# Two-layer hybrid encoder in one kernel on one core: norm products, residual means, weight splits and the last transposes at other places in their engines' queues

## The chip, the core and the metric

The kernel runs on 1 core of one Trainium2 chip. Its engines each work through a queue of their own, in order: TensorE (PE, with its weight loads PEld), VectorE (DVE), ScalarE (ACT), GpSimd (POOL), and SyncE (SP), which issues most DMAs. The metric is the device time of one execution in microseconds (us); lower is better. Before the change the median of 3 runs is 2886.24 us (2885.1 to 2886.93).

## The reference, cut to what matters

Two layers over 1040 tokens (16 meta tokens and 1024 inputs) of width 1024. Layer 0 mixes tokens with a bidirectional S5 scan and a GLU, layer 1 with grouped-query attention. Each mixer is followed by a dense SwiGLU feed-forward part (width 2816), and each of the four parts ends in the same step:

```
x = layer_norm(alpha * x + f(x), gain, bias)      # mean and variance over the 1024 features of a token
```

The output is the last x without the 16 meta tokens.

## The kernel before, in words

Activations lie with features on partitions: `acc[:, k, tokens]` for eight feature tiles k, and 1040 tokens in three token tiles, 0 and 1 of 348 tokens and 2 of 344. Every product is made of three fp32r matmuls, from a high and a low half of both operands (L695, L696, L697); `Hh` and `Hl` are the halves of x, `unit` those of a weight block, `gt` those of the gated hidden values. One product group over eight feature tiles is 24 matmuls, one over the two hidden tiles of a chunk is 6. PSUM has eight banks, drawn from one pool (`bank()`).

The four norms are numbered `ln` 0 to 3: 0 behind the S5 part, 1 behind the first feed-forward part, 2 behind the attention, 3 behind the second feed-forward part, last. A norm works on one token tile. `ln_square` squares each finished feature tile on ACT (L722) and adds it on POOL into two partial sums s and q (`lns`, L724). `layer_norm` sums these over the partitions by two plain fp32 matmuls with a matrix of ones (L736, L737), the sums' products below; then ACT and DVE make the reciprocal root (L707 to L711), and for each feature tile DVE scales x (L751), ACT writes `Hh` (L752), DVE writes `Hl` (L746). After that `residual()` prepares the next residual sum: POOL adds the eight feature tiles (`lnz`, L765), PE makes their mean over partitions (L769), and DVE subtracts it from each feature tile (L772). The mean's bank is held until the eighth subtraction.

Such helper work is a generator. It is recorded between the product groups: each `yield` gives an amount of work, `group_done` counts it down (1.75 for each half of a 24-matmul group, 0.9 for a 6-matmul group), and the next piece is recorded when the count is used up. So the numbers behind `yield` fix where each piece stands in the queues of its engines; `flush` records what is left of a piece at once.

`Weights` streams 512 KB blocks of the weights: `dma` loads `raw`, and `split` turns a block into high and low halves. For most blocks ACT makes the high half (L610) and DVE the low half (L612); `on_pool` gives the low half of four blocks (the k and v weights of the attention) to POOL, also L612. The `down` blocks of a feed-forward part get their row means removed: ACT L607 and L617, DVE L618. `tick` makes the next split when a unit buffer is free.

A feed-forward part runs in eleven chunks: gate and up groups for three token tiles, then eight `down` groups of 6 matmuls for each token tile, whose results DVE adds into `acc` (L880 in the first chunk, L882 in the others). At the end of the program, for each token tile, PE transposes x back in pieces of up to 128 tokens (L1535), DVE and ACT copy a half of each piece into `ot` (L1539, L1537; three buffers), and SP sends it out.

Of the kernel before, what the change touches and what calls it, by code (L numbers as in the profile page):

```python
# [9 lines left out]
FP32 = mybir.dt.float32  # L10
# [3 lines left out]
ALU = mybir.AluOpType  # L14
# [24 lines left out]
class Pools:  # L39


    def __init__(self, tc):
        self.tc = tc
        self.open = {}
# [69 lines left out]
def s5_phase(nc, tc, P, a, ident, acc, xres, ydram, late):  # L114
# [180 lines left out]
    G3 = [tab2.tile([128, T, G], FP32, name=f"G{i}") for i in range(3)]  # L295
    E3 = [tab.tile([128, T, G], FP32, name=f"E{i}") for i in range(3)]
    fw, bw = slice(0, 64), slice(64, 128)
# [77 lines left out]

    def E(c2, g):
        return Eh[2 * g // G][:, c2, g % (G // 2)]
# [42 lines left out]
    def inside(gb):  # L420
# [7 lines left out]
        for j in range(NB):  # L428
            g = NB * gb + j
            for c2, src in enumerate((Br, Bi)):  # L430
                for d in range(2):
                    r = slice(64 * d, 64 * d + 64)
                    PE.matmul(b[32 * d:32 * d + CH, j * 128:(j + 1) * 128], src[r, g],
                              E(c2, g)[r].rearrange("p s c -> p (s c)"), start=(c2 == 0), stop=(c2 == 1))
        yield 6
# [92 lines left out]
    for ft in range(KT):  # L528
        for g0 in range(8 * ft, 8 * ft + 8, 2):
            b = bank()  # L530
            for j in range(2):
                g = g0 + j
                for c2 in range(2):
                    PE.matmul(b[:, j * NK:(j + 1) * NK], E(c2, g).rearrange("p s c -> p (s c)"), XS[:, :, c2, g],  # L534
                              start=(c2 == 0), stop=(c2 == 1))
# [31 lines left out]
class Weights:  # L567


    def __init__(self, nc, n_units, n_raw):  # L570
        self.nc, self.nu, self.nr = nc, n_units, n_raw
        self.src = []
        self.centre = {}
        self.on_pool = set()
        self.raw = []
        self.unit = []
        self.free = []
        self.base = 0
        self.limit = 10 ** 6
# [18 lines left out]
    def split(self):  # L598
        n = len(self.unit)
        self.dma()  # L600
        r = self.raw[n]
        u = self.up[(n - self.base) % self.nu // (self.nu // 2)].tile([128, 2, 1024], FP32R, tag="unit", name="unit")
        A, V = self.nc.scalar, self.nc.vector
        c = self.centre.get(n, False)
        if c is None:
            m = self.rp.tile([128, 1], FP32, tag="mean", name="mean")
            A.activation(out=u[:, 1], in_=r, func=ACTF.Copy, scale=-1.0 / 1024, accum_out=m)  # L607
            c = m
        if c is False:
            A.copy(out=u[:, 0], in_=r)  # L610
            E = self.nc.gpsimd if n in self.on_pool else V
            E.tensor_tensor(out=u[:, 1], in0=r, in1=u[:, 0].bitcast(FP32), op=ALU.subtract)  # L612
        else:
            w = 1024 // c.shape[1]
            for i in range(c.shape[1]):
                x = slice(w * i, w * i + w)
                A.activation(out=u[:, 0, x], in_=r[:, x], func=ACTF.Identity, bias=c[:, i:i + 1])  # L617
                V.scalar_tensor_tensor(out=u[:, 1, x], in0=r[:, x], scalar=c[:, i:i + 1], in1=u[:, 0, x].bitcast(FP32),  # L618
                                       op0=ALU.add, op1=ALU.subtract)
        self.unit.append(u)  # L620
        self.dma()

    def tick(self):
        n = len(self.unit)
        if n < min(len(self.src), self.limit) and (n < self.nu or self.free[n - self.nu]):
            self.split()

# [26 lines left out]
class Net:  # L654
    def __init__(self, nc, tc, P, a):
        self.nc, self.tc, self.P, self.a = nc, tc, P, a
        self.bg = []
        self.ln_s = {}


# [15 lines left out]
    def start(self, gen, key):  # L676
        it = [gen, 0, key]
        self.bg.append(it)
        self.bg_step(it)
        return it  # L680

    def flush(self, key):
        for it in list(self.bg):
            while it[2] == key and it in self.bg:
                self.bg_step(it)
# [40 lines left out]
    def layer_norm(self, tok, ln, last=False, save=None):  # L726
        nc = self.nc
        V, A, PE, PO = nc.vector, nc.scalar, nc.tensor, nc.gpsimd
        t0, n = TOK[tok]
        acc = self.acc  # L730
        x = [acc[:, k, t0:t0 + n] for k in range(KT)]
        tp = self.ln_p
        s, q2 = self.ln_s[tok, 0], self.ln_s[tok, 1]
        yield (3,3,3)[tok] if ln == 1 else 3.0
        v = self.bank()[:, :n]
        PE.matmul(v, self.ones, s, start=True, stop=False)  # L736
        PE.matmul(v, self.ones, q2, start=False, stop=True)  # L737
        A.preload_act_table_set("natural_log_exp_and_others")
        u = self.rstd(v, self.eps_ln, n, tp)

        def bias(k):
            return self.small[:, 32 + 8 * ln + k:32 + 8 * ln + k + 1]

        def finish(k):
            if not last:
                V.scalar_tensor_tensor(out=self.Hl[:, k, t0:t0 + n], in0=x[k], scalar=bias(k),  # L746
                                       in1=self.Hh[:, k, t0:t0 + n].bitcast(FP32), op0=ALU.add, op1=ALU.subtract)

        for k in range(KT):
            g = self.small[:, 8 * ln + k:8 * ln + k + 1]  # L750
            V.scalar_tensor_tensor(out=x[k], in0=x[k], scalar=g, in1=u, op0=ALU.mult, op1=ALU.mult)  # L751
            A.activation(out=x[k] if last else self.Hh[:, k, t0:t0 + n], in_=x[k], func=ACTF.Identity, bias=bias(k))  # L752
            if k > 1:
                finish(k - 2)
            if k % 2:
                yield 1.8
        finish(KT - 2)
        finish(KT - 1)

        def residual():  # L760

            yield (20.,20.,20.)[tok] if ln == 1 else 28.0
            sz = tp.tile([128, 348], FP32, tag="s", name="lnz", bufs=2)[:, :n]
            for k in range(1, KT):
                PO.tensor_tensor(out=sz, in0=x[0] if k == 1 else sz, in1=x[k], op=ALU.add)  # L765
                yield 0.9
            yield 4.0
            mz = self.bank()[:, :n]
            PE.matmul(mz, self.ones, sz, start=True, stop=True)  # L769
            for k in range(KT):  # L770
                b = self.bias_c[:, 8 * ln + k:8 * ln + k + 1]
                V.scalar_tensor_tensor(out=x[k], in0=x[k], scalar=b, in1=mz, op0=ALU.add, op1=ALU.subtract)  # L772
                yield 0.9
            if save is not None:
                nc.gpsimd.dma_start(out=save.rearrange("(k p) t -> p k t", p=128)[:, :, t0:t0 + n],
                                    in_=acc[:, :, t0:t0 + n])

        if not last:
            self.start(residual(), ("lnb", tok))
# [452 lines left out]
def whole(nc, tc, a, out):  # L1232
    P = Pools(tc)
    N = Net(nc, tc, P, a)
    V, A, PE, PO = nc.vector, nc.scalar, nc.tensor, nc.gpsimd
# [18 lines left out]
    w = N.w = Weights(nc, NU, NR)  # L1254
# [13 lines left out]
    wq = a["attn_w_qkv"][0]  # L1268
    uk = N.add_square(wq, 1024)
    uv = N.add_square(wq, 1280)  # L1270
    w.on_pool.update((uk + uv)[:4])
    uq = [N.add_square(wq, 256 * i) for i in range(2)]
    uv2 = N.add_square(wq, 1280)
    uq += [N.add_square(wq, 256 * i) for i in range(2, 4)]
# [250 lines left out]
    for t in range(3):  # L1525
        N.flush(("ln", t))
        t0, n = TOK[t]
        c0 = max(t0, 16)
        while c0 < t0 + n:
            m = min(128, t0 + n - c0)  # L1530
            ot = outp.tile([128, D], FP32, tag="ot", name="ot")
            for h in range(2):
                b = N.bank()
                for f in range(4):
                    PE.transpose(b[:m, f * 128:(f + 1) * 128], acc[:, 4 * h + f, c0:c0 + m], ident)  # L1535
                if h:
                    A.copy(out=ot[:m, 512:], in_=b[:m])  # L1537
                else:
                    V.tensor_copy(out=ot[:m, :512], in_=b[:m])  # L1539
            nc.sync.dma_start(out=out[0, c0 - 16:c0 - 16 + m, :], in_=ot[:m])  # L1540
            c0 += m
# [48 lines left out]
```

## Time and profile before

| | |
|---|---|
| median of 3 runs | 2886.24 us |
| the profiled execution | 2882.8 us, its span 2881.0 us |
| PE busy share of the span | 92% |
| DVE, ACT, POOL busy share | 55%, 41%, 19% |
| mean granted TensorE clock | 0.962 |

Times of the trace count from the start of the span. The S5 part ends at about 329 us, its output products and norm 0 at about 530, the first feed-forward part at about 1288, the attention at about 2000, the second feed-forward part at about 2845. A granted clock of 0.5 is the lower of TensorE's two levels (1.2 GHz), 1.0 the upper (2.4 GHz).

### The profile page before, as it was taken

Reading aid. Unit: us, or ns where it says so; the run is one execution under the profiler, and the core shown is the slowest. Engines: PE = TensorE matmul, PEld = TensorE weight load, DVE = VectorE, ACT = ScalarE, POOL = GpSimd, SP = SyncE. Lnnn points to the kernel's source line nnn. Section 1 sums busy time; section 2 is a strip of 40 time slices with the busy share of each in tenths; the row PEclk is TensorE's granted clock in tenths of the full one; section 3 lists DMA queues with packets and bytes.
Section 4 is the critical chain, followed back from the end, with each engine's and each line's share of the span. In section 5 each row is a group of like instructions: output and inputs, shape, how many; then the busy total and the mean of one; then the engine's idle time right before and its main releaser. Section 6 shows DMA issues by size and latency. Waiting matters only on the chain.

```text
span 2881.0 us, 43478 instructions
## 1 busy us (share of the span) xinstructions
PE 2660.3 (92%) x17277; PEld 2560.6 (89%) x17277; DVE 1586.5 (55%) x3270; ACT 1168.4 (41%) x2170; POOL 545.2 (19%) x544
## 2 busy tenths in 40 slices
PE   6654999999999999998999998999999999999997
PEld 5544899999999999998988888888999999999996
DVE  8897353743333333338768888886473333333334
ACT  6545442532212221244558777775432121222225
POOL 3771142400000000024014443431230000000002
PEclk8776999999999999999999999999999999999998
DMA  5111664121111111101201011112111111111101
GB/s 131 28 36 31 192 208 148 52 81 45 45 45 52 52 52 52 45 30 65 99 12 41 21 38 49 23 23 90 34 47 45 51 44 52 45 45 45 44 30 59
DMA packets 124839, 167.44 MB, mean 58 GB/s; under 512 B 13499, under 2 KB 104971, under 8 KB 124635
## 3 DMA queue, kind: packets, MB, share of 16 engines
q1 hardware_dynamic: 118203, 141.22, 17.2%
q0 software_dynamic: 5712, 21.30, 2.2%
q8 instruction: 136, 2.23, 0.3%
q10 hardware_dynamic: 720, 2.13, 0.2%
q14 instruction: 68, 0.56, 0.1%
HBM read 126.41 MB, written 21.23 MB: 51 GB/s over the span
## 4 chain that ended last, share of the span: by engine, by line
PE 77%; DVE 14%; ACT 4%; issue 3%; DMA 1%; POOL 1%; SPq 0%; ACTq 0%; POOLq 0%; DVEq 0%
PE bk L696 21%; PE bk L695 21%; PE bk L697 21%; PE pv L1107 4%; PE pt L1085 3%; DVE mx L1065 2%; DVE pl L1098 2%; PE b L534 2%; DVE IN L509 2%; DVE TA L507 2%; DVE XS L511 2%; ACT ph L1093 1%; DVE acc L751 1%; ACT P L1069 1%; PE bk L917 1%
## 5 line engine op out<-in xcount | busy, mean ns | idle before, releaser
L695 PE MATMUL bk<-Hh,unit 128*128 128x348 f32 (+1 forms) x2928 | 956.1, 327 | 7.4 <-ACT Hh L785 3.8
L696 PE MATMUL bk<-Hl,unit 128*128 128x348 f32 (+1 forms) x2928 | 945.3, 323 | 1.3 <-DVE Hl L789 1.0
L697 PE MATMUL bk<-Hh,unit 128*128 128x348 f32 (+1 forms) x2928 | 943.7, 322 | 0.0
L695 PEld LDWEIGHTS bk<-Hh,unit 128*128 128x128 f32 x2928 | 555.1, 190 | 12.6 <-ACT vf L1477 3.8
L696 PEld LDWEIGHTS bk<-Hl,unit 128*128 128x128 f32 x2928 | 554.8, 189 | 6.8 <-DVE Hl L789 2.4
L697 PEld LDWEIGHTS bk<-Hh,unit 128*128 128x128 f32 x2928 | 554.7, 189 | 0.0
L859 DVE TENSOR_TENSOR sg<-sg,bk 128x348 f32<-128x348 f32 x132 | 68.0, 515 | 631.7 <-PE bk L697 623.9
L724 POOL TENSOR_TENSOR lns<-lns,lnsq 128x348 f32<-128x348 f32 (+1 forms) x72 | 70.0, 982 | 1550.9 <-ACT lnsq L722 1549.8
L695 PE MATMUL bk<-gt,unit 128*128 128x348 f32 (+1 forms) x1056 | 340.3, 322 | 0.0
L697 PE MATMUL bk<-gt,unit 128*128 128x348 f32 (+1 forms) x1056 | 338.9, 321 | 0.0
L696 PE MATMUL bk<-gt,unit 128*128 128x348 f32 (+1 forms) x1056 | 338.3, 320 | 0.0
L882 DVE TENSOR_TENSOR acc<-acc,bk 128x348 f32<-128x348 f32 (+1 forms) x480 | 237.3, 512 | 112.5 <-PE bk L697 112.5
L861 ACT CAST gt<-sg 128x348 fp32r<-128x348 f32 x132 | 63.6, 482 | 490.0 <-DVE sg L859 490.0
L1085 PE MATMUL pt<-ident,P 128*116 128x128 f32 (+1 forms) x1188 | 181.6, 279 | 44.0 <-DVE pl L1098 38.7
L1098 DVE TENSOR_TENSOR pl<-pt,ph 116x512 fp32r<-116x512 f32 (+3 forms) x340 | 204.2, 618 | 15.1 <-ACT ph L1093 13.1
L1073 POOL TENSOR_SCALAR P<-P,l 128x1044 f32<-128x1044 f32 x132 | 149.9, 1148 | 293.3 <-PE pv L1107 170.0
L1085 PEld LDWEIGHTS pt<-ident,P 128*116 128x116 f32 (+1 forms) x1188 | 132.7, 136 | 80.5 <-issue 32.4
L696 PEld LDWEIGHTS bk<-gt,unit 128*128 128x128 f32 x1056 | 198.7, 188 | 0.5 <-issue 0.2
L695 PEld LDWEIGHTS bk<-gt,unit 128*128 128x128 f32 x1056 | 198.7, 188 | 0.5 <-issue 0.2
L610 ACT CAST unit<-raw 128x1024 fp32r<-128x1024 f32 x110 | 113.1, 1046 | 211.1 <-DMA raw<-in_ffn_w_up_dram 166.2
L1093 ACT CAST ph<-pt 116x512 fp32r<-116x512 f32 (+3 forms) x340 | 168.7, 535 | 73.9 <-PE pt L1085 59.8
L697 PEld LDWEIGHTS bk<-gt,unit 128*128 128x128 f32 x1056 | 198.6, 188 | 0.0
(286 smaller groups left out, 4053.7 us busy)
## 6 DMA issues: line engine op xcount, KB each, us to landing
raw<-in_ffn_w_gate_dram SPq DMA_DIRECT2D x44, 512.0 KB
raw<-in_ffn_w_up_dram SPq DMA_DIRECT2D x44, 512.0 KB
raw<-in_ffn_w_down_dram SPq DMA_DIRECT2D x44, 512.0 KB
y<-xdram SPq DMA_DIRECT2D x16, 520.0 KB
QA<-QH SPq DMA_DIRECT2D x30, 260.0 KB
raw<-in_attn_w_qkv_dram SPq DMA_DIRECT2D x14, 512.0 KB
xdram<-acc SPq DMA_DIRECT2D x32, 130.0 KB
xres<-xn POOLq DMA_DIRECT2D x8, 520.0 KB, 5.1
```

The source lines that it names most:

```text
L610: A.copy(out=u[:, 0], in_=r)
L695: mm(out, wh, xh, start=(first and i == 0), stop=False)
L696: mm(out, wh, xl, start=False, stop=False)
L697: mm(out, wl, xh, start=False, stop=(last and i == n - 1))
L724: (nc.vector if on_dve else nc.gpsimd).tensor_tensor(out=part, in0=part, in1=sq, op=ALU.add)
L859: V.tensor_tensor(out=sg, in0=sg, in1=bu, op=ALU.mult)
L882: V.tensor_tensor(out=x, in0=x, in1=b, op=ALU.add)
L1073: PO.tensor_scalar(out=k.P, in0=k.P, scalar1=k.l, scalar2=1.0, op0=ALU.mult, op1=ALU.mult)
L1085: PE.transpose(b[:m, w * i + 128 * x:w * i + 128 * x + 128], u.P[x][:, KB_N * kt:KB_N * kt + m], self.ident)
L1093: A.copy(out=u.ph[s][:m, :w], in_=u.t[s][:m, :w])
L1098: V.tensor_tensor(out=u.pl[s][:m, :w], in0=u.t[s][:m, :w], in1=u.ph[s][:m, :w].bitcast(FP32), op=ALU.subtract)
L1107: PE.matmul(u.o[:, :u.w], VAs[u.j][:m, kt], (u.ph, u.pl)[x][s][:m, c:c + u.w], start=(kt == 0 and x == 0), stop=(kt == KBS - 1 and x == 1))
```

## The change

Six edits. The sums' products of token tile 2 come later: norms 0 and 2 wait for 7.0 units of work in place of 3.0 (24 matmuls further on), norms 1 and 3 for 5.0 (12 matmuls further on). While norm tile 2 waits for these products, `hold` keeps `tick` from splitting a `down` block. The residual mean starts after 46, 38 and 28 units for tiles 0, 1, 2 of norms 0 and 2 (28 each before), and after 28, 26 and 22 for norm 1 (20 each before). The four low halves on POOL go to DVE. In the last stage `begin` records the sums' products of tile 2 behind the first piece of tile 1, in place of behind its third.

```diff
@@ class Weights
-        self.on_pool = set()
+        self.hold = False
@@ split
-            E = self.nc.gpsimd if n in self.on_pool else V
-            E.tensor_tensor(out=u[:, 1], in0=r, in1=u[:, 0].bitcast(FP32), op=ALU.subtract)
+            V.tensor_tensor(out=u[:, 1], in0=r, in1=u[:, 0].bitcast(FP32), op=ALU.subtract)
@@ tick
         n = len(self.unit)
+        if self.hold and n in self.centre and self.centre[n] is None:
+            return
@@ class Net
+        self.begun = []
...
+    def begin(self, key):
+
+        for it in list(self.bg):
+            if it[2] == key and it[1] > 0 and it not in self.begun:
+                self.begun.append(it)
+                self.bg_step(it)
@@ layer_norm
-        yield (3,3,3)[tok] if ln == 1 else 3.0
+        self.w.hold = tok == 2
+        yield 3.0 if tok < 2 else 5.0 if ln % 2 else 7.0
         v = self.bank()[:, :n]
         PE.matmul(v, self.ones, s, start=True, stop=False)
         PE.matmul(v, self.ones, q2, start=False, stop=True)
         A.preload_act_table_set("natural_log_exp_and_others")
         u = self.rstd(v, self.eps_ln, n, tp)
+        self.w.hold = False
@@ residual
-            yield (20.,20.,20.)[tok] if ln == 1 else 28.0
+            yield ((46.0, 38.0, 28.0), (28.0, 26.0, 22.0))[ln % 2][tok]
@@ whole
-    w.on_pool.update((uk + uv)[:4])
@@ the last stage
         while c0 < t0 + n:
+            if t == 1 and c0 > t0:
+                N.begin(("ln", 2))
```

On ACT, at the start of the first feed-forward part (the second starts alike), the rows before are these; `unit,mean` is the row mean of a `down` block, `rs_y` and `rs_u` belong to the norm of tile 2 (344 tokens), `sg` and `gt` to the gate of tile 0 (348):

```order
L607 ACTIVATE unit,mean<-raw 128x1024
L617 ACTIVATE unit<-raw,mean 128x1024
L607 ACTIVATE unit,mean<-raw 128x1024
L617 ACTIVATE unit<-raw,mean 128x1024
L738 ACT_TABLE_LOAD
L707 ACTIVATE rs_y<-bk,eps_ln 128x344
L708 ACTIVATE rs_y<-rs_y 128x344
L709 ACTIVATE rs_u<-rs_y 128x344
L752 ACTIVATE Hh<-acc,small 128x344 x4
```

and in the changed kernel:

```order
L607 ACTIVATE unit,mean<-raw 128x1024
L616 ACTIVATE unit<-raw,mean 128x1024
L869 ACT_TABLE_LOAD
L869 ACTIVATE sg<-bk 128x348
L872 CAST gt<-sg 128x348
L748 ACT_TABLE_LOAD
L716 ACTIVATE rs_y<-bk,eps_ln 128x344
L717 ACTIVATE rs_y<-rs_y 128x344
L718 ACTIVATE rs_u<-rs_y 128x344
L763 ACTIVATE Hh<-acc,small 128x344 x2
L607 ACTIVATE unit,mean<-raw 128x1024
L616 ACTIVATE unit<-raw,mean 128x1024
```

The first gate and up groups now stand ahead of the norm of tile 2, with a table load of their own, and the second `down` block is split behind its first `Hh`.

On DVE, where the first `down` groups of that part begin (`acc<-acc,bias_c,bk` is a subtraction of the residual mean, `acc<-acc,bk` the addition of a `down` result), the rows before are:

```order
L772 SCALAR_TENSOR_TENSOR acc<-acc,bias_c,bk 128x348 x7
L859 TENSOR_TENSOR sg<-sg,bk 128x344
L862 TENSOR_TENSOR gt<-sg,gt 128x344
L772 SCALAR_TENSOR_TENSOR acc<-acc,bias_c,bk 128x348
L880 SCALAR_TENSOR_TENSOR acc<-acc,bk 128x348 x4
L612 TENSOR_TENSOR unit<-raw,unit 128x1024
L880 SCALAR_TENSOR_TENSOR acc<-acc,bk 128x348 x4
L612 TENSOR_TENSOR unit<-raw,unit 128x1024
```

and in the changed kernel:

```order
L783 SCALAR_TENSOR_TENSOR acc<-acc,bias_c,bk 128x348 x2
L870 TENSOR_TENSOR sg<-sg,bk 128x344
L873 TENSOR_TENSOR gt<-sg,gt 128x344
L783 SCALAR_TENSOR_TENSOR acc<-acc,bias_c,bk 128x348 x6
L891 SCALAR_TENSOR_TENSOR acc<-acc,bk 128x348 x4
L611 TENSOR_TENSOR unit<-raw,unit 128x1024
L783 SCALAR_TENSOR_TENSOR acc<-acc,bias_c,bk 128x348
L891 SCALAR_TENSOR_TENSOR acc<-acc,bk 128x348
L783 SCALAR_TENSOR_TENSOR acc<-acc,bias_c,bk 128x348
```

The subtractions of tile 0 move from the gate and up groups to the head of the `down` groups, and those of tile 1 stand among the `down` results: between the last `sg` of the gates and the `down` results of tile 2 there are 22 subtractions, where there were 9.

On ACT, at the end of the program, the rows before are these (`ot` are output pieces of token tile 1, the rest the norm of tile 2):

```order
L752 ACTIVATE acc<-acc,small 128x348 x2
L1537 COPY ot<-bk 128x512 x2
L1537 COPY ot<-bk 92x512
L738 ACT_TABLE_LOAD
L707 ACTIVATE rs_y<-bk,eps_ln 128x344
L708 ACTIVATE rs_y<-rs_y 128x344
L709 ACTIVATE rs_u<-rs_y 128x344
L752 ACTIVATE acc<-acc,small 128x344 x8
```

and in the changed kernel:

```order
L763 ACTIVATE acc<-acc,small 128x348 x2
L1549 COPY ot<-bk 128x512
L748 ACT_TABLE_LOAD
L716 ACTIVATE rs_y<-bk,eps_ln 128x344
L717 ACTIVATE rs_y<-rs_y 128x344
L718 ACTIVATE rs_u<-rs_y 128x344
L763 ACTIVATE acc<-acc,small 128x344 x2
L1549 COPY ot<-bk 128x512
L1549 COPY ot<-bk 92x512
L763 ACTIVATE acc<-acc,small 128x344 x6
```

The second and third piece's copies of tile 1 move from ahead of the norm of tile 2 to behind its second feature tile.

## Rows read from the trace of the kernel before

**Rows 1.** The page, part 1: busy time and share of each engine.

```profile
PE 2660.3 (92%) x17277; PEld 2560.6 (89%) x17277; DVE 1586.5 (55%) x3270; ACT 1168.4 (41%) x2170; POOL 545.2 (19%) x544
```

**Rows 2.** Waits of PE: line, waited for, us in total, times, longest.

```profile
PE bk L736 <- POOL lns L724: 11.7, 4, 4.7
...
PE bk L737 <- POOL lns L724: 6.7, 2, 3.3
...
PE bk L695 <- ACT vf L1477: 3.6, 1, 3.6
...
PE bk L696 <- DVE Hl L789: 1.0, 1, 1.0
```

**Rows 3.** Short windows: length, busy us of PE, PEld, DVE, ACT, POOL; granted clock.

```profile
330.20:333.60 3.40, 3.40 (x12) 3.40 (x13) 3.40 (x7) 3.40 (x8) 1.38 (x4) 0.50 0.77 97
...
388.20:391.60 3.40, 3.40 (x20) 3.00 (x19) 2.08 (x6) 2.49 (x7) 0.78 (x1) 1.00 0.62 173
538.40:541.80 3.40, 3.40 (x11) 2.92 (x11) 2.04 (x2) 3.35 (x5) 3.24 (x3) 0.50 0.03 7
...
1330.30:1337.10 6.80, 5.62 (x19) 5.62 (x20) 5.74 (x13) 4.25 (x10) 0.00 (x0) 0.50 0.00 1
2088.00:2094.80 6.80, 5.21 (x16) 4.74 (x17) 3.19 (x2) 6.68 (x9) 5.95 (x5) 0.50 0.30 90
```

**Rows 4.** Timeline of PE at the mean of x: start, us, instruction, idle before.

```profile
387.48 0.85 PE L1369 MATMUL bk<-sx,ones 128*128 128x348 f32 x2 [0.95 <-POOL sx L1362]
```

**Rows 5.** Timeline at the start of the first feed-forward part.

```profile
533.98 0.85 PE L736 MATMUL bk<-lns,ones 128*128 128x344 f32 x2 [1.20 <-POOL lns L724]
...
535.97 0.50 DVE L1398 SCALAR_TENSOR_TENSOR acc<-acc,bk 128x344 f32<-128x344 f32 x1
...
537.20 0.91 POOL L724 TENSOR_TENSOR lns<-lns,lnsq 128x344 f32<-128x344 f32 x1 [3.27 <-ACT lnsq L722]
...
538.16 1.34 PE L737 MATMUL bk<-lns,ones 128*128 128x344 f32 x2 [3.33 <-POOL lns L724]
```

**Rows 6.** Timeline: the end of norm 0, and the first product that reads it.

```profile
559.43 1.54 DVE L746 SCALAR_TENSOR_TENSOR Hl<-acc,small,Hh 128x344 fp32r<-128x344 f32 x3
...
567.77 0.32 PE L695 MATMUL bk<-Hh,unit 128*128 128x344 f32 x1
```

**Rows 7.** Windows by stage, columns as in rows 3.

```profile
583.40:606.80 23.40, 23.40 (x149) 23.20 (x148) 20.24 (x38) 6.57 (x9) 0.00 (x0) 1.00 0.41 137
...
1331.50:1400.00 68.50, 68.50 (x395) 63.73 (x396) 57.49 (x104) 34.45 (x70) 18.10 (x19) 0.96 0.31 101
```

**Rows 8.** Timeline of DVE where the first down groups begin.

```profile
585.19 0.57 DVE L772 SCALAR_TENSOR_TENSOR acc<-acc,bias_c,bk 128x348 f32<-128x348 f32 x1
585.68 1.36 DVE L880 SCALAR_TENSOR_TENSOR acc<-acc,bk 128x348 f32<-128x348 f32 x3
```

**Rows 9.** Timeline: low halves on DVE and POOL, norm 1, and the vf copy.

```profile
526.71 1.23 DVE L612 TENSOR_TENSOR unit<-raw,unit 128x1024 fp32r<-128x1024 f32 x1 [1.55 <-ACT unit L610]
...
1301.82 2.65 POOL L612 TENSOR_TENSOR unit<-raw,unit 128x1024 fp32r<-128x1024 f32 x1
...
1308.15 1.51 PE L736 MATMUL bk<-lns,ones 128*128 128x344 f32 x2 [4.54 <-POOL lns L724]
...
1331.07 0.35 ACT L1477 COPY vf<-bk 116x256 f32<-116x256 f32 x1
```

**Rows 10.** The chain that ended last, in the last stage.

```profile
2855.14 7.46 DMA out_dram<-ot
```

**Rows 11.** Timeline of the last stage.

```profile
2856.01 3.98 PE L1535 MATMUL bk<-ident,acc 128*128 128x128 f32 x18 [1.81 <-ACT acc L752]
...
2862.70 0.58 ACT L1537 COPY ot<-bk 92x512 f32<-92x512 f32 x1 [3.35 <-DMA out_dram<-ot]
2863.30 1.28 ACT L738 ACT_TABLE_LOAD   x1
...
2867.38 3.99 DVE L751 SCALAR_TENSOR_TENSOR acc<-acc,small,rs_u 128x344 f32<-128x344 f32 x8
```

## The prediction

> **What bounds the kernel now.** I read the page's busy shares first: PE is busy 2660.3 of 2881.0 us [rows 1], so only the holes of PE and the stretches at its lower clock can be won. The waits of PE then name the holes that the change touches. The sums' products wait for POOL's partial sums, 11.7 + 6.7 us in all, and one product waits 3.6 us for ACT's copy of `vf` [rows 2]. The timelines place them: 1.20 + 3.33 us at 534 [rows 5], as much again at the second feed-forward part, 4.7 us for norm 1's tile 1, 4.54 us for its tile 2 (11.7 = 1.2 + 1.2 + 4.7 + 4.5 and 6.7 = 3.3 + 3.3), and 3.6 us for `vf` behind that [rows 2, 9]. Short windows show the second price of a hole: behind the wait at 534 the granted clock is 0.50 for 3.4 us, behind its twin 6.8 us, behind the `vf` wait 6.8 us [rows 3], and each us at 0.50 loses half a us. Behind a wait of 0.95 us the clock stays 1.00 [rows 3, 4]; behind one of 1.0 us that follows another short one it falls [rows 2, 3]. The last stage is a chain of its own: a DMA of 7.46 us frees an `ot` buffer, a copy follows, and only behind that copy ACT starts the last norm [rows 10, 11].
>
> **Start of each feed-forward part (twice).** What releases the second sums' product is not moved: DVE's last addition ends at 536.5, POOL's last add at 538.1 [rows 5]. Between the last product of the part before and the sums there are now 48 matmuls in place of 24. 24 matmuls at full clock are 3.8 us (149 in 23.40 us are 0.157 us each [rows 7]). So of 1.20 + 3.33 = 4.53 us about 0.7 us is left. A wait of 0.7 us is below the 0.95 us behind which the clock stayed, so the 3.4 us at half clock go too and give back 1.7 us. Gain: 3.8 + 1.7 = 5.5 us. At the twin 6.8 us were lost to the clock; I count one 3.4 us stretch there as well, and keep the other 1.7 us for the range.
>
> The cover for the norm of tile 2 is the gate and up work of tiles 0 and 1. It ended at 559.43 + 1.54 = 561.0 and was first read at 567.77 [rows 6]. PE now comes to that read some 5.5 us earlier, at 562.3, and to its eighth feature tile 3.3 us later. So about 4.6 us of cover are left for ACT's and DVE's detours: a first gate's `sg` and `gt` ahead of the norm, and a table load of 1.28 us [rows 11] for it. I cost these at nothing.
>
> The Trainium skill speaks against that step: ScalarE: Activation LUTs, section Table sets: the hidden batching unit, wants activations batched by table set, and the change splits a batch, two loads of 1.28 us per part. The trace agrees with the price of a load and shows the cover above; what it would take if the cover failed is the third rival.
>
> **First `down` groups (twice).** Here the change takes back. From 583.40 to 606.80 DVE was busy 20.24 of 23.40 us [rows 7], with 9 subtractions of the residual mean; in the changed order the same stretch holds 22. One takes 585.68 - 585.19 = 0.49 us from start to start [rows 8], so DVE has 20.24 + 13 x 0.49 = 26.6 us of work in 23.4 us, 3.2 us too much. POOL's adds and the mean's product are earlier than these subtractions and are not the limit. Eight PSUM banks let PE run ahead, but a mean's bank stays held until its eighth subtraction, which is now the last thing on DVE ahead of tile 2's results. Ends: 0 (the banks cover it) and 3.2 + 1.7 = 4.9 us (waits over 1 us, and a stretch at half clock). I take 3.2 us, the overrun itself. Net per part: 5.5 - 3.2 = 2.3 us; two parts: 4.6 us.
>
> **Norm 1 and the k, v and q products.** The sums' products of tile 2 move 12 matmuls on, 1.9 us of PE work into a wait of 4.54 us [rows 9]. The mean of tile 0 moves 62 matmuls on and leaves its bank free for one product more, 3.8 us of work in front of the wait for `vf`. That copy also has two `Hh` of tile 2 fewer ahead of it, so the 3.62 us go, with 3.4 us for the clock [rows 2, 3, 9]. Gains: 1.9 + 3.6 + 3.4 = 8.9 us.
>
> Against that stand the four low halves. On POOL one takes 2.65 us at its longest and delays the partial sums; on DVE it takes 1.23 us, but DVE first stands idle 1.55 us for ACT's high half, with the `down` results and norm steps queued behind it [rows 9]. In the queue of tile 2's sums that is 2.8 us on DVE for 2.65 us on POOL, about even; for tile 1 too. I count 1.4 us of loss, one half's run behind the last result. Then DVE must catch up: from 1331.50 to 1400.00 it is busy 57.49 of 68.50 us [rows 7], and its work does not begin earlier, since norm 1's sums are ready no sooner. A PE that comes 7.5 us earlier meets that queue. Of 7.5 us I keep 2.0 us, about what the shift of the sums gives by itself. Ends: a loss as in the fourth rival, and the full 7.5 us.
>
> **The last stage.** 16 transposes of the second and third piece now stand behind the sums' products: of 18 in 3.98 us [rows 11], 16 x 0.21 = 3.3 us by the mean of the row. The sums then run at half clock, 2.7 us for four passes where two took 1.34 us [rows 5]: from 2859.99 - 3.3 = 2856.7 to 2859.4. More comes from ACT: the root starts there, at about 2859.4, no longer at 2863.30 + 1.28 = 2864.6 behind the copy that waits for the DMA. DVE's first scaling follows 2.8 us later (2867.38 - 2864.6), at 2862.2. Two feature tiles, 1.0 us; then two copies into `ot` of 0.6 us each, the second of which is free at 2862.6; then six tiles at 0.5 us: 2867.4, where it was 2867.38 + 3.99 = 2871.4. Gain: 4.0 us. The two copies also start their DMAs later; if one takes 7.46 us again [rows 10], the last copy waits about 1.5 us. I take 3.5 us; ends 1.0 and 5.2 us (2864.6 - 2859.4).
>
> **Sum.** 4.6 + 2.0 + 3.5 = 10.1 us. The profiled execution took 2882.8 us (span 2881.0 and 1.8 us around it), so it would take 2872.7. The median of the runs shown lies 3.4 us above the profiled execution; the same offset gives 2876.1, and I predict 2876.
>
> **Rivals.**
> 1. The subtractions eat the gain. Both feed-forward parts lose 4.9 of their 5.5 us, norm 1 gives nothing, the last stage 2.2 us: 3.4 us, 2882.8. For it: DVE's 26.6 us against 23.4. Against: eight banks of lead.
> 2. All comes in full: 5.5 and 7.2 us, no overrun, 7.5 us in norm 1, 5.2 us at the end: 25.4 us, 2861. Against: DVE's 57.49 of 68.50 us, and the overrun.
> 3. The norm of tile 2 is late at the new place. Two loads of 1.28 us per part beyond the cover of 4.6 us cost 2.6 us twice: 10.1 - 5.2 = 4.9 us, 2881.3. Against: the cover.
> 4. Slower. The four low halves block DVE: each 1.55 + 1.23 = 2.8 us, together 11.1 us in front of the `down` results on which both waits of norm 1 hang, and each wait, then over 7 us, is followed by a further 3.4 us lost to the clock: 17.9 us. With 8.1 us won elsewhere this is 9.8 us slower, 2896. It decides if POOL's relief (four times up to 2.65 us) doesn't shorten the waits; below about 8 us of exposed halves the whole is not slower. Against: both waits end on POOL.
> That a step doesn't take effect I see nowhere: the orders of ACT and DVE show each.
>
> **How the numbers follow.** Forecast 0.64, rival 1 0.16, rival 2 0.09, rival 3 0.05, rival 4 0.06. The forecast's own spread is 2869 to 2882: the overrun 0 or 4.9 us in both parts, norm 1 and the end towards their ends. A measurement of this kernel can tell 0.2%, 5.8 us, from no change, so 2880.5 is the border. Faster: 0.60 of the forecast, rival 2 and 0.02 of rival 3, 0.71. Same: the other 0.04 of the forecast, rival 1 and 0.03 of rival 3, 0.23. Slower: 0.06. The range 2866 to 2884 leaves out rival 4, rival 2 and a rest of the forecast, together under 0.2.
>
> **What would show it.** In the profile after: a wait below 1 us at each feed-forward part's sums and a clock of 1.00 behind it; short waits of PE for DVE (the subtractions) some 70 us later; no wait for `vf`; waits of around 4 us left at norm 1; the last wait of PE 4 us shorter, and no DMA in front of the last norm. I am wrong if the wait at the sums keeps over 2 us, if PE waits over 5 us in the first `down` groups, or if norm 1's waits grow.

## The result

Six runs of each kernel on one chip: the changed kernel takes 2871.07 us (2868.7 to 2874.99), the kernel before 2886.59 us (2880.97 to 2888.21); the ratio is 0.995 with a 95% interval of 0.9938 to 0.9963. A later comparison (five runs against nine) gave 2869.21 us and 0.9939 (0.9927 to 0.9952). So the change saves about 15.5 us where 10 were forecast: faster, below the forecast of 2876 and inside its range, 2866 to 2884.

### The profile after

The page of the changed kernel, part 1 (compare [rows 1]): PE has 5.9 us less of busy time (time at half clock counts as busy) and the span is 14.1 us shorter.

```profile
PE 2654.4 (93%) x17277; PEld 2553.5 (89%) x17277; DVE 1590.5 (55%) x3274; ACT 1170.4 (41%) x2172; POOL 554.8 (19%) x540
```

Line numbers have moved: the sums' products are L746 and L747, the low and high products L704 to L706, the residual subtraction L783, the norm's `Hl` L757. The waits of PE that answer to [rows 2] (line, waited for, us in total, times, longest):

```profile
PE bk L746 <- POOL lns L733: 8.1, 2, 4.4
...
PE bk L928 <- ACT rsq L925: 5.0, 2, 3.0
...
PE bk L704 <- DVE acc L783: 1.5, 2, 0.8
...
PE bk L747 <- POOL lns L733: 1.2, 2, 0.6
```

Both waits of 1.2 us and both of 3.3 us are gone, 0.6 us is left of each pair, and the wait for `vf` is gone. New are two waits of 0.8 us for the residual subtraction, and two behind norm 1 for the rotary step (`rsq`), of 2.0 and 3.0 us. The places, in the timeline of the changed kernel (start, us, instruction, idle before):

```profile
541.58 0.85 PE L747 MATMUL bk<-lns,ones 128*128 128x344 f32 x2 [0.60 <-POOL lns L733]
...
566.62 1.54 DVE L757 SCALAR_TENSOR_TENSOR Hl<-acc,small,Hh 128x344 fp32r<-128x344 f32 x3
...
579.22 0.94 POOL L776 TENSOR_TENSOR lnz<-acc 128x344 f32<-128x344 f32 x1 [21.30 <-PE bk L780]
580.24 6.28 POOL L776 TENSOR_TENSOR lnz<-lnz,acc 128x344 f32<-128x344 f32 x6
...
582.62 3.01 DVE L783 SCALAR_TENSOR_TENSOR acc<-acc,bias_c,bk 128x348 f32<-128x348 f32 x6
...
604.82 0.42 PE L704 MATMUL bk<-gt,unit 128*128 128x344 f32 x1 [0.78 <-DVE acc L783]
...
1377.40 0.91 POOL L786 DMA_DIRECT2D hres<-acc  x1 [11.66 <-DVE acc L783]
...
1384.33 0.52 DVE L935 SCALAR_TENSOR_TENSOR acc<-rraw,rs_u 128x348 f32<-128x348 f32 x1 [1.65 <-DMA hres<-acc]
...
1385.40 0.85 PE L928 MATMUL bk<-rsq,blk 128*128 128x344 f32 x2 [3.04 <-ACT rsq L925]
```

Windows of the changed kernel (length, busy us of PE, PEld, DVE, ACT, POOL, granted clock, DMA share, GB/s), to be read beside [rows 3, 7]: the clock keeps 1.00 at the feed-forward start, and in the first `down` groups DVE is all but saturated, 23.33 of 24.00 us.

```profile
538.40:541.80 3.40, 2.66 (x13) 2.11 (x14) 1.49 (x4) 1.78 (x4) 1.18 (x2) 1.00 0.47 159
541.80:545.20 3.40, 3.40 (x21) 3.20 (x21) 2.29 (x2) 2.79 (x4) 3.24 (x3) 1.00 0.00 0
581.00:605.00 24.00, 23.22 (x144) 22.44 (x143) 23.33 (x45) 6.57 (x9) 5.13 (x6) 1.00 0.36 113
```

The last stage, where [rows 11] had the table load behind a copy that waited 3.35 us for a DMA: the load now follows a copy that waits for no DMA, the sums run meanwhile, 16 transposes stand behind them, and the eight feature tiles are scaled in two pieces.

```profile
2847.23 1.28 ACT L748 ACT_TABLE_LOAD   x1
2847.53 1.35 PE L747 MATMUL bk<-lns,ones 128*128 128x344 f32 x2
2848.68 3.28 PE L1547 MATMUL bk<-ident,acc 128*128 128x128 f32 x16
...
2851.71 1.06 DVE L762 SCALAR_TENSOR_TENSOR acc<-acc,small,rs_u 128x344 f32<-128x344 f32 x2
...
2853.89 3.00 DVE L762 SCALAR_TENSOR_TENSOR acc<-acc,small,rs_u 128x344 f32<-128x344 f32 x6
```

### Where the time went, by stage

Every kernel here issues the same 4056 product triples in one order, so the start of the k-th triple can be compared between traces. The table takes the changed kernel's triples at the times named, and gives how many us more than the changed kernel each kernel took from one to the other.

| kernel (profiled execution) | first feed-forward start, 530 to 620 | norm 1, 1280 to 1395 | second start, 2075 to 2165 | last stage, 2835 to the end |
|---|---|---|---|---|
| before | 4.25 | 2.63 | 5.32 | 3.68 |
| sums of tile 2 undone | 6.86 | 2.34 | 7.15 | -0.67 |
| means undone | 3.46 | 2.31 | 3.38 | -0.01 |
| norm 1's means earlier | -0.01 | 0.31 | 0.00 | -0.18 |
| `begin` undone | 0.01 | 2.46 | -0.01 | 3.95 |
| POOL adds | 8.79 | 1.31 | 7.81 | 0.14 |
| more DVE work | 3.31 | 2.60 | 4.87 | -0.06 |
| `hold` undone | -0.01 | 1.35 | -0.01 | -0.18 |
| norm 1's sums later | -0.01 | 0.69 | -0.01 | -0.01 |
| halves on POOL | -0.01 | 0.27 | 0.00 | -0.17 |
| tiles 1 and 2 earlier | 0.01 | -1.59 | -0.03 | -0.01 |
| all means | -1.11 | -0.54 | -0.96 | 0.01 |
| changed, again | 0.00 | -0.03 | -0.02 | -0.16 |

Rows whose edit lies elsewhere show what a column can tell: 0.03 us in the two feed-forward columns, 0.2 us in the last stage (with one miss of 0.67: the first edit moves nothing there either, since `begin` sets the place of those sums), but -0.03 to 2.60 us at norm 1, where the edits `begin`, `hold`, POOL adds and more DVE work change nothing. Between the columns, stretches that the change doesn't touch differ as well: up to 430 us the kernel before was 3.4 us ahead of the changed one, in the attention it lost 1.6 us. So 4.25 + 2.63 + 5.32 + 3.68 - 3.4 + 1.6 = 14.1 us, the difference of the spans.

### The profile page after: what moved, and what is told of

It reads as the page before. It is cut to its first block, busy times and chain, and to the rows that moved or that the text cites. A ratio compares the mean times of both kernels' runs of the same rounds, so it can differ in the third digit from the quotient of the medians.

```text
span 2866.9 us, 43502 instructions
## 1 busy us (share of the span) xinstructions
PE 2654.4 (93%) x17277; PEld 2553.5 (89%) x17277; DVE 1590.5 (55%) x3274; ACT 1170.4 (41%) x2172; POOL 554.8 (19%) x540
## 3 DMA queue, kind: packets, MB, share of 16 engines
q0 software_dynamic: 5712, 21.30, 2.2%
## 4 chain that ended last, share of the span: by engine, by line
PE 74%; DVE 16%; ACT 5%; issue 3%; DMA 2%; SPq 1%; POOL 0%; ACTq 0%; DVEq 0%; POOLq 0%
PE bk L704 21%; PE bk L705 21%; PE bk L706 21%; PE pv L1118 4%; PE pt L1096 3%; DVE mx L1076 3%; DVE pl L1109 2%; PE b L534 2%; DVE IN L509 2%; DVE TA L507 2%; DVE XS L511 2%; ACT ph L1104 1%; ACT P L1080 1%; DVE acc L783 1%; DVE acc L762 1%
## 5 line engine op out<-in xcount | busy, mean ns | idle before, releaser
L704 PE MATMUL bk<-Hh,unit 128*128 128x348 f32 (+1 forms) x2928 | 953.3, 326 | 6.1 <-ACT Hh L796 6.1
L706 PE MATMUL bk<-Hh,unit 128*128 128x348 f32 (+1 forms) x2928 | 941.6, 322 | 0.3
L704 PEld LDWEIGHTS bk<-Hh,unit 128*128 128x128 f32 x2928 | 553.0, 189 | 11.0 <-ACT Hh L796 5.7
L706 PEld LDWEIGHTS bk<-Hh,unit 128*128 128x128 f32 x2928 | 552.8, 189 | 0.9 <-DVE unit L611 0.9
L704 PE MATMUL bk<-gt,unit 128*128 128x348 f32 (+1 forms) x1056 | 341.0, 323 | 1.5 <-DVE acc L783 1.5
L706 PE MATMUL bk<-gt,unit 128*128 128x348 f32 (+1 forms) x1056 | 339.1, 321 | 0.0
L704 PEld LDWEIGHTS bk<-gt,unit 128*128 128x128 f32 x1056 | 198.9, 188 | 3.1 <-DVE acc L783 2.6
L706 PEld LDWEIGHTS bk<-gt,unit 128*128 128x128 f32 x1056 | 198.8, 188 | 0.0
```

Of the source, the lines that this page charges most:

```text
L704: mm(out, wh, xh, start=(first and i == 0), stop=False)
L706: mm(out, wl, xh, start=False, stop=(last and i == n - 1))
```

## The experiments

**Is it the sums? Undo their place (e1).**

```diff
-        yield 3.0 if tok < 2 else 5.0 if ln % 2 else 7.0
+        yield 3.0
```

> The changed kernel with one edit undone: the sums' products of token tile 2 wait for 3.0 units again in all four norms. Theory (the 24 matmuls that now stand ahead of them give the two feed-forward starts their gain): the waits of 1.2 + 3.3 us for POOL's partial sums are back at 534 us and at its twin near 2083 us, with 3.4 to 6.8 us of half clock behind each; the waits of 0.78 and 0.72 us in the first down groups are gone, since PE comes later; norm 1's wait for tile 2 stays within 1 us of 4.4. In all 8 to 11 us slower than the changed kernel (2871.1): 2879 to 2882. Rival (the place of the residual means gives the gain, by taking subtractions out of DVE's queue in the gate and up groups): the waits for POOL are short or are given back within the part; less than 3 us slower, 2871 to 2874.

Measured: 2886.58 us (2881.09 to 2889.67), ratio to before 1.0003 (0.9993 to 1.0012). The waits of PE are those of the kernel before again:

```profile
PE bk L746 <- POOL lns L733: 12.7, 4, 6.5
PE bk L747 <- POOL lns L733: 6.7, 2, 3.3
...
PE bk L704 <- DVE acc L783: 2.0, 2, 1.0
```

The theory holds for the waits for POOL, but the loss is 15.5 us, not 8 to 11, and three of its points were wrong: the waits in the `down` groups stay (1.03 and 0.94 us), norm 1's wait for tile 2 grows from 4.38 to 6.51 us ("within 1 us of 4.4"), and the feed-forward starts are 2.6 and 1.8 us slower than in the kernel before. The late means without the later sums are a loss. Of the 2.6 us, some 0.8 are clock: the half clock at the first start lasts 6.8 us in this execution, with 5.04 us of busy time, and 3.4 us in the kernel before [rows 3], so 2.5 us are lost to it in place of 1.7.

**Undo the place of the means (e2).**

```diff
-            yield ((46.0, 38.0, 28.0), (28.0, 26.0, 22.0))[ln % 2][tok]
+            yield ((28.0, 28.0, 28.0), (20.0, 20.0, 20.0))[ln % 2][tok]
```

> The changed kernel with one edit undone: the residual means start after 28 units (norms 0 and 2) and 20 units (norm 1) again. Theory (22 subtractions among the first down results cost PE two waits of 0.78 and 0.72 us, no more; norm 1's later means free a bank for the product that waits for vf, and cost a wait of 3.0 us later, for the save of tile 2): the waits at 604 and 2147 us go, 1.5 us faster; the wait for vf is back with 2 to 3.6 us and some half clock behind it, and the 3.0 us wait at 1382 us goes. In all within 3 us of the changed kernel: 2870 to 2874. Rival (my forecast's term: the subtractions overrun DVE by 3.2 us in each part, hidden in the changed kernel somewhere in the following chunks): 5 us or more faster than the changed kernel, under 2866. Second rival (the earlier subtractions now stand in DVE's queue ahead of the norm of tile 2, which itself comes later): PE waits 1 us or more for Hl or gt between 545 and 585 us, 3 us or more slower per part, 2877 or more.

Measured: 2876.84 us (2873.7 to 2880.48), 0.9966 (0.9953 to 0.9979). The theory's figure (within 3 us of the changed kernel) missed, and the waits and, within 0.2 us, the time of the second rival came: the waits in the `down` groups go, but PE waits for the norm of tile 2 in the gate and up groups of both parts (2.3 us in the first, with 3.4 us at half clock behind it). The rival's mechanism did not: between 538 and 573 us no subtraction (L783) stands on DVE in this run. At norm 1 the wait for `vf` is back, and of the rotary step's waits the one at 1382 us is gone, as expected.

```profile
PE bk L705 <- DVE Hl L757: 4.3, 5, 1.1
PE bk L704 <- ACT vf L1487: 3.6, 1, 3.6
...
PE bk L928 <- ACT rsq L925: 1.3, 1, 1.3
```

So neither move does it alone: against the kernel before, the sums alone (this run) give 0.8 and 1.9 us at the two starts, the means alone (e1) cost 2.6 (with the clock named there) and 1.8, both together give 4.25 and 5.32. (The other edits that both runs still hold are worth nothing at these places, see e7 and e9.) The timeline of this run suggests why, and the next experiment tests it: POOL adds almost without a pause beside the norm of tile 2, and of DVE's 16 operations for it nine take over 1 us (three in the changed kernel), 1.24 us where they took 0.56.

```profile
551.82 7.19 POOL L776 TENSOR_TENSOR lnz<-lnz,acc 128x348 f32<-128x348 f32 x6
559.43 1.24 POOL L776 TENSOR_TENSOR lnz<-acc 128x344 f32<-128x344 f32 x1 [0.42 <-DVE acc L762]
560.75 2.24 POOL L776 TENSOR_TENSOR lnz<-lnz,acc 128x344 f32<-128x344 f32 x2
...
559.79 1.25 DVE L762 SCALAR_TENSOR_TENSOR acc<-acc,small,rs_u 128x344 f32<-128x344 f32 x1
560.96 1.24 DVE L757 SCALAR_TENSOR_TENSOR Hl<-acc,small,Hh 128x344 fp32r<-128x344 f32 x1
```

In the changed kernel the adds of tile 2 wait until the later mean of tile 0 has read its `lnz` buffer (the row at 579.22 above, 21.30 us of idle POOL), and by then the norm is over.

**Put POOL beside the norm and change nothing else (e5).** Sixteen adds on a scratch tile, no order on PE, DVE or ACT changed.

```diff
         u = self.rstd(v, self.eps_ln, n, tp)
+        if tok == 2 and ln in (0, 2):
...
+            PO.memset(dz, 0.0)
+            for _ in range(16):
+                PO.tensor_tensor(out=dz, in0=dz, in1=u, op=ALU.add)
```

> The changed kernel with 16 useless POOL adds (SBUF to SBUF, 128x344) behind the root of norm tile 2, in both feed-forward starts; every order on PE, DVE and ACT is unchanged. Theory (the earlier residual means of the run before cost PE its waits for Hl because POOL's adds then ran beside the norm of tile 2, and DVE's operations with two SBUF inputs took 1.24 us in place of 0.56 beside them): DVE's scalings and Hl between 558 and 568 us take 1.2 us each, the last Hl of tile 2 comes 4 us later or more, PE waits 2 to 6 us for Hl at 565 to 575 us and at its twin near 2110 us; 2878 to 2886. Rival (it was the place of the subtractions in DVE's queue, or the banks of the means): DVE's operations keep 0.56 us and PE doesn't wait; 2871, no change.

Measured: 2884.57 us (2879.27 to 2890.21), 0.9998 (0.9989 to 1.0008): the whole gain is lost again, 8.79 and 7.81 us in the two starts, more than they had won. The windows of `Hl` on DVE (busy us, times, clock), in the changed kernel

```profile
549.00:576.00 27.00, 4.35 (x8) 1.00 0.22 78
```

in this run

```profile
549.00:576.00 27.00, 9.75 (x8) 0.93 0.17 59
```

and its wait of PE:

```profile
PE bk L705 <- DVE Hl L760: 10.1, 4, 3.7
```

0.54 us each against 1.22. The theory holds, and the rival is out; the time lies inside its 2878 to 2886. The Trainium skill, SBUF — State Buffer, section Who interferes with whom, has the rule: a VectorE instruction with two SBUF inputs contends with a GpSimd instruction that reads SBUF. By that rule the residual subtraction, whose second input is in PSUM, should not be slowed; the trace agrees: beside POOL's adds at 580 to 586 us, in the timeline of the changed kernel above, six subtractions take 3.01 us, 0.50 us each.

**Is the overrun of DVE in the `down` groups real? Add to it (e6).** Six useless additions of about 0.5 us among the first `down` results of tile 1.

```diff
+                    if t == 1 and o < 6:
...
+                        V.tensor_tensor(out=dz, in0=x, in1=x, op=ALU.add)
```

> The changed kernel with six useless DVE additions (128x348, about 0.5 us each) among the down results of tile 1 in the first chunk of each feed-forward part: 2.9 us more for DVE in the stretch that my forecast said overruns by 3.2 us. Theory (the overrun is there, but the eight banks let PE run 2.4 us ahead of DVE, and in the changed kernel only 0.78 and 0.72 us of it reach PE; this lead is used up): the waits at 604 and 2147 us grow by the full 2.9 us to 3.5 us each, with half clock behind them: 5.8 us of waits and up to 3.4 us for the clock, 2877 to 2880. Rival (the waits at 604 and 2147 us come from the place of tile 2's mean, not from DVE's load): the waits stay under 1.5 us and the time within 2 us of 2871.

Measured: 2881.6 us (2878.86 to 2885.4), 0.9988 (0.9978 to 0.9997). The waits are these, 2.8 us for the subtraction and 0.5 + 0.2 us for the `down` results in each part, where 0.8 stood:

```profile
PE bk L704 <- DVE acc L783: 5.6, 2, 2.8
...
PE bk L704 <- DVE acc L891: 1.5, 4, 0.5
```

2.9 us of work gave 2.8 us more of wait (3.54 for 0.78 in the first part): DVE is the limit there, and the lead of the banks is used up in the changed kernel. At norm 1 the profiled execution lost 2.6 us that the edit doesn't explain, and the total lies 1.6 us above the expectation; the two starts (3.31 and 4.87 us, with half clock behind the second) are the measure.

**Undo `begin` (e4).**

```diff
-                N.begin(("ln", 2))
+                pass
```

> The changed kernel without begin: in the last stage the sums' products of token tile 2 stand behind the third piece of tile 1 again. Theory: nothing changes before 2839 us; ACT's root stands behind the copy that waits for the output DMA again, PE's last wait is some 7 us, and the lead falls by 4 us: 2875. Rival (the gain of the last stage came from PE's earlier arrival or from the clock, not from the place): less than 1.5 us slower, 2871 to 2872.5.

Measured: 2873.35 us (2872.5 to 2874.61), 0.9955 (0.994 to 0.997). The last stage alone is 3.95 us longer, and PE's last wait is the old one:

```profile
2860.86 6.50 PE L1547 MATMUL bk<-ident,acc 128*128 128x128 f32 x24 [7.29 <-ACT acc L763]
```

By the stage the theory holds to 0.1 us; the total was 1.7 us better than expected, within what the untouched stretches move.

**Undo `hold` (e7).**

```diff
-        self.w.hold = tok == 2
+        self.w.hold = False
```

> The changed kernel without hold: the second down block is split ahead of the norm of tile 2 (ACT 2.4 us, DVE 1.8 us) and not between its second and third feature tile, where DVE now stands idle 2.88 us for ACT. Theory (the norm has cover, and what counts is when its eighth Hl is done): the norm starts some 2 us later but is not interrupted, and ends within 1 us of where it did; PE does not wait; within 1.5 us of the changed kernel, 2870 to 2873. Rival (the cover is used up by then): PE waits 1 to 3 us for Hl between 560 and 572 us and at its twin; 2874 to 2879.

Measured: 2872.79 us (2867.63 to 2874.72), 0.9952 (0.9937 to 0.9967). Both starts agree with the changed kernel to 0.01 us: `hold` is worth nothing here.

**Put the four low halves back on POOL (e9).** The edit restores `on_pool` and its line in `split`.

> The changed kernel with one edit undone: the four low halves of the k and v weights are on POOL again. Theory (my forecast: about even, a loss or gain of at most 1.4 us): the waits for POOL's partial sums at norm 1 grow by about 1 us at tile 1 (3.8 to 4.7, as in the kernel before) and by less at tile 2, and DVE's relief gives it back behind them; 2870 to 2873, and within 1.5 us by the time that PE reaches 1400 us. Rival (my forecast's fourth: on DVE the halves stand ahead of the down results): both waits shrink by 1 us or more with the halves back on POOL; 2866 to 2869.

Measured: 2871.49 us (2870.54 to 2873.2), 0.9953 (0.994 to 0.9967); 0.27 us at norm 1. The first wait there is 4.70 us, as in the kernel before, the second only 2.48 (they are 3.77 and 4.38 in the changed kernel), and a rotary wait grows from 1.97 to 3.26. From the end of the first wait to the end of the second it is 15.07 us here and 16.94 in the changed kernel. So on DVE the halves make tile 1's sums ready 0.93 us earlier and tile 2's 0.94 us later, less than the 1.4 us of loss that the forecast counted, and the fourth rival's 11.1 us are out. That the move as a whole is even, as forecast, is as much as this column can tell.

**Norm 1: three variants of its places (e3, e8, e10).** First the means earlier, `(24.0, 22.0, 18.0)` for norm 1:

> The changed kernel, but norm 1's residual means start after 24, 22 and 18 units instead of 28, 26 and 22 (20 each in the kernel before). Theory (PE's wait of 3.03 us at 1382 us is a write-after-read chain: DVE's rotary result may overwrite x of tile 2 only when the save of x to hres has read it, and the save starts behind the eighth subtraction): the save starts some 8 us earlier, the wait goes, and the lead that norm 1 gains stays: 3 us faster than the changed kernel, 2868, unless the wait for vf returns (then PE waits 1 to 3.6 us at 1328 us and it is even). Rival (DVE's queue is the limit there, 57.5 of 68.5 us busy, and takes any lead back): another wait of 2 to 3 us, for DVE, stands in the same stretch; no change, 2871.

Measured: 2867.69 us (2866.83 to 2870.86), 0.9939 (0.9922 to 0.9955). The wait at 1382 us is gone, but in place of it the mean of tile 0, now 36 matmuls earlier, waits for the bank that `vf` holds, with half clock behind it:

```profile
PE bk L780 <- ACT vf L1487: 1.8, 1, 1.8
```

Norm 1 as a whole is even (0.31 us), as the expectation said for this case; in the profiled execution the lower time comes from stretches that the edit doesn't touch, 1.6 us of it before 430 us. One detail of the expectation was wrong: the save that DVE waits for is tile 1's (128x348, sent at 1377.40), not tile 2's. Next, the sums later still, 6.6 units for tile 1 and 8.5 for tile 2, with means at 28, 24 and 18:

> A further step from the changed kernel, at norm 1 only: the sums' products of tile 1 wait for 6.6 units in place of 3.0 and those of tile 2 for 8.5 in place of 5.0 (24 matmuls further on, each), and its residual means start after 28, 24 and 18 units. Theory (as at the feed-forward starts, matmuls moved ahead of the sums fill PE's wait for POOL): the waits of 3.8 us at 1288 us and 4.4 us at 1304 us shrink below 1 us and the half clock behind them goes, 8 to 10 us at first; DVE's queue (57.5 of 68.5 us) takes part of it back; 2863 to 2868. Rival (all of it is taken back, since norm 1's tiles are then late for the k and v products): waits for Hl or vf between 1310 and 1345 us, no gain; 2870 to 2874.

Measured: 2871.25 us (2869.0 to 2874.87), 0.9951 (0.9936 to 0.9965): no gain, the rival's outcome, though not by its waits for `Hl` or `vf`. The waits for POOL at norm 1 are gone and PE is 6.0 us ahead at 1325 us, 0.7 us behind at 1395, since the rotary steps that hang on the later norms now wait:

```profile
PE bk L928 <- ACT rsq L925: 9.5, 3, 4.6
```

Then tile 0's mean left where the change has it, tiles 1 and 2 earlier, `(28.0, 22.0, 18.0)`:

> The changed kernel, but norm 1's residual means of tiles 1 and 2 start after 22 and 18 units (26 and 22), and that of tile 0 stays at 28. Theory (the wait of 3.03 us at 1382 us is DVE's write to x of tile 1 waiting for the save of tile 1, which leaves behind its eighth subtraction at 1377; the wait for vf, which came back in the run with tile 0 at 24, hangs on tile 0's mean and its bank alone): neither wait is there; 2.5 to 3.5 us faster than the changed kernel by the time that PE reaches 1400 us, 2868. Rival (DVE's queue, 57.5 of 68.5 us, takes it back): other waits of 2 to 3 us in the stretch; no change.

Measured: 2865.88 us (2862.54 to 2871.74), 0.9935 (0.9923 to 0.9948). Neither wait is there; of the rotary waits the first is left:

```profile
PE bk L928 <- ACT rsq L925: 2.3, 1, 2.3
```

Norm 1 is 1.59 us shorter than in the changed kernel's own profile, less than the 2.5 to 3.5 expected, and below all the runs that leave norm 1 alone (-0.03 to 2.60). By the triples it gains 3.2 us between 1380 and 1390 us, as expected, and had come there 1.6 us late, in part by 6.8 us of half clock behind the second sums where the changed kernel had 3.4; e3 gains 3.3 us at the same place. So the wait at 1382 us hung on the later means of tiles 1 and 2, not on tile 0's; of these two it is tile 1's by the trace of the changed kernel, since the write that waits has 348 columns and the save sent at 1377.40 is the second of three.

**All means at the best places found (e11)**, `(40.0, 34.0, 28.0)` for norms 0 and 2 besides, **and the changed kernel again (e12).**

> As the run with norm 1's residual means after 28, 22 and 18 units, and besides norms 0 and 2 with 40, 34 and 28 units (46, 38, 28 in the changed kernel, 28 each before): about 17 subtractions in place of 22 behind the last gate, and tile 2's POOL adds, which wait for the mean of tile 0, begin some 6 us earlier, still behind the norm of tile 2 (its last Hl is done at 568 us). Theory (the cost of 0.78 and 0.72 us is DVE's load among the down results, the cost of an early mean is POOL beside the norm): both waits go and no wait for Hl comes: 1.5 us faster than that run, 2866.5. Rival (there is no room between the two: POOL meets the gates' DVE work): waits for Hl or gt of 1 us or more; 2869 to 2873.

> The changed kernel as it is, on the same chip as the runs beside it. Every theory: 2871, within 3 us.

Measured: 2866.05 us (2862.37 to 2872.46), 0.9937 (0.9923 to 0.9951), beside 2869.21 us (2862.22 to 2871.52) of the changed kernel. The waits for the subtraction are gone at both starts, no wait for `Hl` came, and the starts are 1.11 and 0.96 us shorter, a little more than the 1.5 us expected of both. The total is that of e10 nevertheless, since norm 1 took 1.05 us more in this execution. Against the changed kernel beside them e10 and e11 are some 3 us faster, inside the spread of either: these totals can't tell it, the stages do.

## Why the prediction was right, and where not

- **Wait and clock at the feed-forward starts** (5.5 us): right, though on a condition that I had not seen (the later means, below). 0.60 us of wait is left where 0.7 was forecast, the clock stays at 1.00 behind it, and 3.9 us of wait and 1.7 us of clock are gone at the first start.
- **The overrun in the `down` groups** ("I take 3.2 us, the overrun itself"): this step failed, by its size. The load was counted rightly (DVE 23.33 of 24.00 us), but PE ran ahead on the banks and waited only 0.78 and 0.72 us; there added work then came through almost in full (e6). The lower end, 0, was the nearer one. With 0.75 us for 3.2 the two starts come to 4.75 each; measured 4.25 and 5.32. The second was higher since its half clock had lasted 6.8 us with 5.21 us of busy time [rows 3], 2.6 us lost in place of 1.7: 3.9 + 2.6 - 0.7 = 5.8 us. Some 0.5 us in each I can't place.
- **The later means** were priced as a cost alone. That they clear POOL out of the norm of tile 2 I did not see: the gain of 5.5 us, and the cover that I "cost at nothing", hold only with them (e2: 3.4 us lost per part). The sum was right there because both edits are in the change, which was luck and not my reason.
- **The cover for the norm of tile 2** ("I cost these at nothing"): nothing came of it, but narrowly. Its eighth `Hl` is done at about 568.1 us (the row at 566.62 above), and PE's first product that reads it starts at 568.65. So of the 4.6 us of cover about 0.5 is left: the detours took some 4 us, not nothing.
- **Norm 1** (2.0 us): measured 2.63, in a column that moves from -0.03 to 2.60 us between executions that share the changed kernel's norm 1. Against the mean of these six, 1.3 us, the kernel before is 1.3 us slower: neither the size nor, safely, the sign can be read. The mechanism can. `vf` went, and the waits left are around 4 us, as forecast. The shift of tile 2's sums was worth 2.1 us (6.51 us of wait without it in e1, 4.38 with it; 1.9 forecast), and the low halves took 0.94 us of it back (e9). PE's lead on the kernel before was 6.2 us at 1380 us and 2.6 at 1390. It was taken back by a wait for the save of tile 1 behind its later subtractions, which I had not named (e10), not by DVE's queue as such. Where the sums are moved further, the rotary steps wait instead (e8).
- **The last stage** (3.5 us): right, 3.68 and 3.95 us (e4).
- **The total** came out 5.4 us below the forecast's difference: 2.0 and 3.0 us by the two starts and some 0.8 by norm 1 and the last stage, in the profiled executions. That is 5.8 us; the difference of 0.4 is less than the untouched stretches move.
- **Rivals**: the first and second did not come: the subtractions cost under 0.8 us per part, and norm 1 gave back most of its lead. The third (the norm late behind two table loads) did not come; PE never waits for tile 2's `Hl` in the changed kernel. Its two loads were one too many: the trace holds 22 table loads where the kernel before has 20, one more per part, since there too a gate's load stood inside this norm. But its result, a late norm, was the near miss, and with early means it comes, through POOL. The fourth is out (e9).

## What to carry to other kernels

When work is moved to fill a wait, look at what then runs beside the chain that the wait stood for: here a sum moved by 24 matmuls won 4 to 5 us only because another edit kept POOL's additions away from the norm's DVE operations. An overrun of one engine is not yet a wait of another: count the buffers between them first, then see whether more load comes through. And where a result is saved by a DMA, the next write to the same place waits for it: give the earliest-overwritten tile its save first.

## What the runs showed of the hardware

- DVE operations with two SBUF inputs took 0.54 us in the changed kernel and 1.22 us beside back-to-back POOL additions (e5); operations with a PSUM input kept their time (0.50 us each beside additions). There the one that started second paid: in the changed kernel `gt<-sg,gt` started at 582.18 us and took 0.52 us, and the POOL addition that started 0.07 us later took 1.25 us, the others there 0.92 to 0.94.
- The same wait was not always followed by the lower clock. At 1382 us the changed kernel's 3.04 us were followed by 1.00; in e6, with the same code there, the same wait of 3.04 us by 0.50:

```profile
1385.40:1388.80 3.40, 3.40 (x18) 3.00 (x19) 3.37 (x7) 1.53 (x3) 1.51 (x2) 1.00 0.44 140
```

```profile
1389.30:1392.60 3.30, 3.30 (x8) 2.34 (x9) 3.27 (x7) 1.53 (x3) 1.44 (x2) 0.50 0.49 141
```

  The first window is the changed kernel's, the second e6's: 18 matmuls against 8 in about the same time. The repeated changed kernel (3.05 us of wait there, -0.03 in norm 1's column) has clock 1.00 behind this wait; e4, e5, e6 and e7 (2.91 to 3.05 us of wait, 1.31 to 2.60 in the column) have 0.50. So the clock goes a long way to explain why that column moves by up to 2.6 us.
- A stage without such waits repeats to 0.03 us between kernels, while the totals of the changed kernel spread over 6 to 9 us. Effects of 1 us can be read by stage where the medians can't tell them.
